# Layer 1's sliding-window attention: how many query panels are projected ahead of it, and how their split operands are laid out

## The chip, the cores and the metric

The kernel runs on one core of a Trainium2 chip. The core has five engines with instruction streams of their own, each in order: the tensor engine (PE), the vector engine (DVE), the scalar engine (ACT), GpSimd (POOL) and SyncE (SP), which here only starts transfers. The metric is the device time of one execution in microseconds (us). Lines are called L528 and so on; they are those of the kernel before unless the text says otherwise.

## The reference, cut to what matters

Two transformer layers over 512 latent tokens and 256 context tokens of width 1024, in float32. The change touches the attention of layer 1, which in the reference reads:

```python
def odd_mixer(a_lat, a_ctx, rows, cols, w_in, sinks, w_out, ctx_out):
    ...
    q, k, v = split(a_lat @ w_in, s)
    q = axial_rope(q, rows, cols)
    k = axial_rope(k, rows, cols)
    qc, kc, vc = split(a_ctx @ w_in, n_ctx)
    o_lat, o_ctx = swa_heads(q, k, v, qc, kc, vc, sinks, ctx_out)
    return o_lat @ w_out, (o_ctx @ w_out if ctx_out else None)
```

`w_in` gives 16 query heads of 64 columns, 2 key heads and 2 value heads; each key head serves 8 query heads. A latent query sees the latent keys within 128 positions and all 256 context keys in one softmax that also has a sink logit per head.

## The kernel before

**Arithmetic.** PE multiplies in a short format. So every operand is split in two: a high part (a cast, on ACT as a rule) and a low part (what the cast lost, a subtract on DVE as a rule). A projection then is three matmuls, high by high, high by low and low by high (L317, L319, L320). Tokens lie along the free dimension and features on the 128 partitions. `wr` is a raw weight panel, `wh` and `wl` its parts (L306, L307).

**The stage.** Before the change's place, layer 1's first products make keys `k32`, values `v32` and the queries of heads 0 and 1, `q0` (L738 to L740, then L317 to L320 for the context). Seven more query panels follow, one for each further pair of heads: `swa_queries(p)` loads 128 columns of `w_in`, multiplies them by the 512 normalised latents (24 matmuls of 512 columns into a `psd` bank), and rotates the result: an ACT copy (L447), a shuffle of partitions on DVE (L448), and three steps on POOL (L450, L451, L452). Then `put_q` splits the panel. A pair's two heads lie on partitions 0 to 63 and 64 to 127. The scores use all 128 rows of PE: for each head an operand `st` holds the high part of its query on its own 64 partitions and the low part on the other 64, and a key operand holds the key on both halves. So `put_q` runs twice over 64 partitions: a cast (L694) and a subtract that writes to the other half (L695). `put_k` makes, for each of the two key heads (`side`), the high operand (L708) and the low operand (L709) on one half and, with `copies` false, computes both again onto the other half (L714, L715); with `copies` true it moves them there by two transfers.

**The attention.** `swa_jobs` gives 16 jobs, two for each of 8 pairs of heads, each with two blocks of 128 queries. In a job each side (head) has scores against the context (4 matmuls of 256 columns into one `pss` bank) and against its window (2 of 256 or 384 columns for each block, L728 and L729). DVE adds the mask and takes the minimum (L538), ACT takes the exponential (L534), PE transposes the weights (L482) into `pst` or `psd` banks, DVE or ACT copies them out (L473, L474), and a run of weighted sums (L528) goes into `pso`, which ACT copies (L612). After a pair, `swa_finish` and `finish_pair` divide by the sums (L1618, L1619, L458, L461, L349, L465). `attend` interleaves the weighted sums of one job with the scores of the next. There are three `s`, two `t`, two `d` banks and one `o` bank; a panel and the transposes share the `d` banks.

**What sets the order.** The kernel is recorded and a scheduler places the instructions on each engine by priority. `beside` puts a generator in a queue of side work, `step` advances that queue by one step, `drain` empties it, and `shifted` lowers the priority of what it records. Here all seven panels are recorded ahead of the attention, 50 places lower (`LQ`), then drained; `EACH` is 0. The scheduler thus sets them near the front and pair 0's first jobs between them. Of the operand tiles `st` there are 12: four for the keys and two for each of four pairs.

## Time and profile before

| | |
|---|---|
| median of 3 runs | 1559.12 us (1555.52 to 1559.58) |
| profiled execution | 1558.19 us |
| its span, first to last instruction | 1556.3 us |
| granted TensorE clock | 0.996 |
| PE, DVE, ACT, POOL busy | 1529.0, 1176.5, 768.0, 217.0 us |
| the attention stage of layer 1, from panel 2 to the output projection | 998.7 to 1147 us |

The page gives, for each engine, the time in which any of its instructions ran. Matmuls overlap in the records: one starts while the last is still draining. So a busy PE can still lose time, and the distance between starts tells more than the busy share. "[0.24 <-ACT st L694]" behind a row says that the engine stood 0.24 us before it and that the cast on L694 let it go. A group's row ends with the same: idle time of the engine just before, and what ended it.

### The profile page before, as it was taken

How to read it: one execution, taken by the hardware profiler on the slowest of the kernel's cores; microseconds unless marked ns; L12 is line 12 of the kernel's file. 1: busy time of each engine (PE TensorE's matmuls, PEld its weight loads, DVE VectorE, ACT ScalarE, POOL GpSimd, SP SyncE). 2: the span in 40 equal slices, each digit the busy share in tenths (PEclk: the TensorE clock that was granted, in tenths of full speed). 3: DMA queues.
4: the chain of work that ended last, by engine and by line, in shares of the span. 5: the costliest groups of instructions: out<-in, count | busy, mean ns of one | idle time of the engine just before them, and what ended most of it. 6: DMA issues, size and time to landing. Idle time of an engine off the chain costs nothing.

```text
span 1556.3 us, 26589 instructions
## 1 busy us (share of the span) xinstructions
PE 1529.0 (98%) x10048; PEld 1374.9 (88%) x10048; DVE 1176.5 (76%) x2408; ACT 768.0 (49%) x1531; POOL 217.0 (14%) x269
## 2 busy tenths in 40 slices
PE   9999999999999999999999999999999999999998
PEld 8788877877999898999999988877789899899998
DVE  4799867676868687777768676789967779678685
ACT  4532677674555242432424335457856455354453
POOL 0021043110101102012021122470012000000001
PEclk9999999999999999999999999999999999999999
DMA  9674632013634545537465494110214223323222
GB/s 321 249 226 142 161 125 65 11 63 138 227 128 139 206 134 182 205 118 288 142 249 187 150 358 139 55 41 1 90 57 167 63 91 126 107 84 131 88 94 89
DMA packets 79073, 219.39 MB, mean 141 GB/s; under 512 B 10720, under 2 KB 17888, under 8 KB 78944
## 3 DMA queue, kind: packets, MB, share of 16 engines
q1 hardware_dynamic: 61280, 147.42, 28.6%
q0 software_dynamic: 16512, 68.69, 12.4%
q8 instruction: 79, 1.29, 0.3%
q10 hardware_dynamic: 1152, 1.57, 0.3%
q14 instruction: 50, 0.41, 0.1%
HBM read 186.97 MB, written 23.07 MB: 135 GB/s over the span
## 4 chain that ended last, share of the span: by engine, by line
PE 88%; DVE 7%; ACT 2%; issue 2%; DMA 1%; POOL 0%; DVEq 0%; ACTq 0%; POOLq 0%
PE pss L1401 5%; PE pss L1400 5%; PE pss L1399 5%; PE pso L528 5%; PE pss L320 4%; PE pss L317 4%; PE pss L319 4%; PE psd L317 4%; PE psd L320 4%; PE psd L319 4%; PE pst L317 3%; PE pst L320 3%; PE pst L319 3%; PE pst L1401 3%; PE pst L1399 3%; PE pst L1400 3%
## 5 line engine op out<-in xcount | busy, mean ns | idle before, releaser
L306 ACT CAST wh<-wr 128x1024 fp32r<-128x1024 f32 (+2 forms) x148 | 115.5, 795 | 224.2 <-DMA wr<-in_w_dn_dram 35.0
L307 DVE TENSOR_TENSOR wl<-wr,wh 128x1024 fp32r<-128x1024 f32 (+2 forms) x145 | 130.9, 910 | 80.6 <-ACT wh L306 76.3
L534 ACT ACTIVATE p<-p,sm 128x512 f32<-128x512 f32 (+3 forms) x144 | 105.0, 730 | 25.8 <-DVE sm L538 25.2
L1399 PE MATMUL pss<-b,wh 128*128 128x384 f32 (+1 forms) x346 | 107.7, 312 | 0.5 <-ACT b L343 0.5
L1400 PE MATMUL pss<-b,wh 128*128 128x384 f32 (+1 forms) x346 | 107.8, 312 | 0.0
L1401 PE MATMUL pss<-b,wl 128*128 128x384 f32 (+1 forms) x346 | 107.0, 311 | 0.0
L319 PE MATMUL psd<-b,wh 128*128 128x512 f32 (+2 forms) x254 | 88.6, 349 | 0.0
L273 DVE CUSTOM_DVE_ANT_0 p<-rope,cond 128x1024 bf16<-128x1024 f32 x64 | 76.8, 1219 | 11.4 <-DMA rope<-in_mod_w_dram 11.2
L317 PE MATMUL psd<-b,wh 128*128 128x512 f32 (+2 forms) x214 | 79.1, 370 | 2.8 <-ACT pl L474 2.2
L528 PE MATMUL pso<-ph,b 128*64 128x256 f32 (+1 forms) x384 | 77.9, 362 | 1.0 <-DVE ph L473 0.9
L528 PE MATMUL pso<-pl,b 128*64 128x256 f32 (+1 forms) x384 | 78.4, 363 | 0.0
L320 PE MATMUL psd<-b,wl 128*128 128x512 f32 (+2 forms) x214 | 77.5, 363 | 0.0
L1401 PE MATMUL pst<-b,wl 128*128 128x384 f32 (+1 forms) x226 | 70.6, 313 | 1.5 <-DVE wl L1387 1.5
L1386 ACT CAST wh<-pl 128x512 fp32r<-128x512 f32 x78 | 44.9, 619 | 53.6 <-PE pss L1400 22.7
L1399 PE MATMUL pst<-b,wh 128*128 128x384 f32 (+1 forms) x226 | 70.7, 313 | 0.6 <-ACT p L1449 0.6
L263 POOL DMA_DIRECT2D rope<-in_mod_w_dram x48 | 25.6, 533 | 323.0 <-DVE mod L273 312.1
L1400 PE MATMUL pst<-b,wh 128*128 128x384 f32 (+1 forms) x226 | 70.5, 312 | 0.0
L1386 ACT CAST wh<-wr 128x1024 fp32r<-128x1024 f32 x39 | 41.0, 1051 | 57.7 <-PE pst L1400 14.8
L319 PE MATMUL pss<-b,wh 128*128 128x256 f32 (+3 forms) x216 | 68.4, 316 | 0.0
L317 PE MATMUL pss<-st,wh 128*128 128x512 f32 (+2 forms) x198 | 67.5, 341 | 0.3 <-ACT wh L306 0.3
L320 PE MATMUL pss<-st,wl 128*128 128x512 f32 (+2 forms) x198 | 67.5, 341 | 0.1
L1399 PEld LDWEIGHTS pss<-b,wh 128*128 128x128 f32 x346 | 65.0, 188 | 1.1 <-ACT b L343 0.8
(606 smaller groups left out, 5290.7 us busy)
## 6 DMA issues: line engine op xcount, KB each, us to landing
wr<-in_w_gu_dram SPq DMA_DIRECT2D x88, 512.0 KB, 4.1
rope<-in_mod_w_dram POOLq DMA_DIRECT2D x48, 512.0 KB, 3.9
wr<-in_w_dn_dram SPq DMA_DIRECT2D x73, 256.0 KB, 2.9
wr<-in_w_out_dram SPq DMA_DIRECT2D x32, 512.0 KB, 3.9
p<-home POOLq DMA_DIRECT2D x40, 384.0 KB, 5.6
home<-p POOLq DMA_DIRECT2D x40, 384.0 KB, 5.9
wr<-in_w_in_dram SPq DMA_DIRECT2D x21, 512.0 KB, 3.9
ph<-in_mod_w_dram SPq DMA_DIRECT2D x24, 256.0 KB, 2.8
```

Of the source, the lines that this page charges most:

```text
L273: behind(V.tensor_tensor_reduce(out=T("p", [P, D], mybir.dt.bfloat16), in0=w, in1=cond[:, v, :], op0=ALU.mult, op1=ALU.add, scale=1.0, sca ...
L306: behind(S.copy(h, r), *after[:1])
L307: behind((G if eng else V).tensor_tensor(lo, r, f(h), op=ALU.subtract), *after[1:])
L317: ins = PE.matmul(o, wh[:, k], mh[:, c], start=first and k == 0, stop=False)
L319: PE.matmul(o, wh[:, k], ml[:, c], start=False, stop=False)
L320: PE.matmul(o, wl[:, k], mh[:, c], start=False, stop=last and k == n - 1)
L528: ins = PE.matmul(o[64 * i : 64 * i + 64, c], v(kt), t, start=n == 0, stop=n == len(moving[i]) - 1)
L534: S.activation(p[:, c], p[:, c], AF.Exp, bias=nm, scale=-1.0, accum_out=dn)
L1386: S.copy(h, t)
L1399: PE.matmul(o, wh, xh, start=first and k == 0, stop=False, skip_group_check=not first)
L1400: PE.matmul(o, wh, xl, start=False, stop=False, skip_group_check=not first)
L1401: PE.matmul(o, wl, xh, start=False, stop=k == 3, skip_group_check=not first)
```

## The change

Three things change together, all in layer 1.

1. Three panels (p = 1 to 3) are recorded ahead of the attention and drained; the other four are put beside it: when `swa_jobs` begins pair p below 4, it puts `swa_queries(p + 4)` into the side work. A pair whose operands are not recorded yet steps the side work until they are.
2. A panel is split once over all 128 partitions: one cast, one subtract in place, and three transfers on SP's queue that bring the halves to the other side.
3. The second key head's operands are recorded behind the three panels, at the lowered priority, and with `copies` true; the first head's stay as they are. Its two transfers go to POOL's queue, since `dense[0]` is true there.

```diff
-LQ, EACH = 50, 0
...
-    def put_k(ks, copies=True, hi=None):
+    def put_k(ks, copies=True, hi=None, only=(0, 1)):
+
+        sides = [(i, ks[i]) for i in only]
...
-            for side, (k1, k2) in enumerate(ks):
+            for side, (k1, k2) in sides:
...
     def swa_queries(p, every=1, get=PQ):
-        q, sets[p] = B(), new_q()
+        q, new = B(), new_q()
         yield from project(I["w_in1"][p], put_rope(q, rope1, SWAP16, scale=0.125), (LATS,), every=every, get=get)
-        put_q(sets[p], None, lo=V.tensor_tensor)(q[:, LATS], LATS)
+        q, (t0, t1) = q[:, LATS], (t[:, LATS] for t in new)
+        up, dn = slice(0, 64), slice(64, 128)
+        S.copy(t0, q)
+        lo = q.bitcast(F32R)
+        V.tensor_tensor(lo, q, f(t0), op=ALU.subtract)
+        dma(t1[up], t0[dn])
+        dma(t1[dn], lo[dn])
+        dma(t0[dn], lo[up])
+        sets[p] = new
...
-    put_k(KS, KC[2])(k32, slice(0, NT))
+    put_k(KS, KC[2], only=(0,))(k32, slice(0, NT))
...
         for p in range(8):
+            while p not in sets:
+                step()
+            if p < 4:
+                beside(swa_queries(p + 4))
             kv = p // 4
...
-    lower[0] = LQ
-    for p in range(1, 8):
+    lower[0] = 50
+    for p in range(1, 4):
         beside(swa_queries(p))
-        if EACH:
-            drain()
-            lower[0] += EACH
     drain()
     lower[0] = LOWER
+    with shifted(LOWER):
+        put_k(KS, only=(1,))(k32, slice(0, NT))
```

The order on all engines is the same ahead of this stage and from the last pair's end on; the number of PE instructions is the same, DVE and ACT have eight fewer each, SP has 21 more transfers and POOL two.

DVE's row where pair 0's attention begins, before. The tiles `b_10337` and `b_10382` are the rotated panels 1 and 2, `pss` the score banks, `wr` a weight panel; L695 are the subtracts over 64 partitions:

```order
L448 STREAM_SHUFFLE b_10417<-b_10416 128x512
L695 TENSOR_TENSOR st_10338<-b_10337,st_10338 64x512
L695 TENSOR_TENSOR st_10339<-b_10337,st_10339 64x512
L538 ISA p_10683,sm_10655<-pss_10675,zeros_92,sink_neg_10161 128x256
...
L307 TENSOR_TENSOR wl_10568<-wr_10565,wh_10567 128x1024
L448 STREAM_SHUFFLE b_10462<-b_10461 128x512
L695 TENSOR_TENSOR st_10383<-b_10382,st_10383 64x512
L695 TENSOR_TENSOR st_10384<-b_10382,st_10384 64x512
L538 ISA p_10683,sm_10655<-pss_10680,nb_10157,sm_10655 128x256
```

The same place after the change, with that kernel's own lines (L537 is L538 of before, L447 is L448, L306 is L307, L472 is L473); L1589 is the subtract over 128 partitions, `b_10333`, `b_10379` and `b_10425` are panels 1 to 3, `pss_10511` and `pss_10516` belong to pair 0's second side and `pss_10536` to its next job:

```order
L447 STREAM_SHUFFLE b_10414<-b_10413 128x512
L1589 TENSOR_TENSOR b_10333<-b_10333,st_10334 128x512
L537 ISA p_10519,sm_10478<-pss_10511,zeros_92,sink_neg_10161 128x256
...
L306 TENSOR_TENSOR wl_11044<-wr_11041,wh_11043 128x1024
L537 ISA p_10519,sm_10478<-pss_10516,nb_10157,sm_10478 128x256
...
L472 COPY ph_10580<-pst_10576 128x384
L1589 TENSOR_TENSOR b_10379<-b_10379,st_10380 128x512
L537 ISA p_10544,sm_10478<-pss_10536,zeros_92,sink_neg_10161 128x256
...
L1589 TENSOR_TENSOR b_10425<-b_10425,st_10426 128x512
L472 COPY pl_10553<-psd_10548 128x512
```

One subtract stands where two stood, and more of pair 0's reductions and copies stand between one panel's subtract and the next.

PE's row after pair 0's first side, before: panel 4 (`psd_10481`) ends, four scores, and panel 5 (`psd_10526`) begins:

```order
L319 MATMUL psd_10481<-b_10093,wh_10477 128x512
L320 MATMUL psd_10481<-b_10092,wl_10478 128x512
L728 MATMUL pss_10680<-st_10165,st_10171 128x256
L729 MATMUL pss_10680<-st_10166,st_10171 128x256
L728 MATMUL pss_10687<-st_10165,st_10171 128x384
L729 MATMUL pss_10687<-st_10166,st_10171 128x384
L317 MATMUL psd_10526<-b_10028,wh_10522 128x512
L319 MATMUL psd_10526<-b_10029,wh_10522 128x512
```

After (L729 and L730 are the scores, L481 the transposes, L316 to L319 the panel), panel 4 is `psd_10507`, and the scores are those of the same side, `pss_10516` and `pss_10526`:

```order
L729 MATMUL pss_10516<-st_10165,st_10171 128x256
L730 MATMUL pss_10516<-st_10166,st_10171 128x256
L316 MATMUL psd_10507<-b_10028,wh_10503 128x512
L318 MATMUL psd_10507<-b_10029,wh_10503 128x512
L729 MATMUL pss_10526<-st_10165,st_10171 128x384
L730 MATMUL pss_10526<-st_10166,st_10171 128x384
L481 MATMUL pst_10555<-ident_r_90,p_10487 128x128
L319 MATMUL psd_10507<-b_10028,wl_10504 128x512
L316 MATMUL psd_10507<-b_10045,wh_10503 128x512
L481 MATMUL pst_10555<-ident_r_90,p_10494 128x128
```

Panels 4 to 7 now stand among scores, transposes and weighted sums, the last of them beside pair 4.

DVE's row late in the attention after the change, beside pair 6, whose score banks are `pss_11737` and `pss_11773`. L464 (L465 of before) finishes a pair, `b_10834`, `b_11052` and `b_11237` being pairs 2, 3 and 4; L306 splits a panel of output weights:

```order
L464 TENSOR_TENSOR b_10834<-b_10834,pst_11644 128x512
L537 ISA p_11745,sm_11676<-pss_11737,zeros_92,sink_neg_10161 128x256
...
L464 TENSOR_TENSOR b_11052<-b_11052,pst_11665 128x512
L1628 TENSOR_TENSOR sm_11238<-sm_11238,sm_11723 128x8
...
L306 TENSOR_TENSOR wl_12193<-wr_12190,wh_12192 128x1024
...
L306 TENSOR_TENSOR wl_12228<-wr_12225,wh_12227 128x1024
L464 TENSOR_TENSOR b_11237<-b_11237,pst_11729 128x512
```

Before, a pair was finished beside the next one; now the finishing steps of pairs 2 to 5 stand in the last three pairs, because they queue behind the panels in the side work.

## The prediction

> **What bounds the kernel now.** I read the page first, then the busy time by stretches of the stage that the change touches, then the tensor engine (PE) instruction by instruction there, then what the vector engine (DVE) does in it. The page's head:
>
> ```profile
> span 1556.3 us, 26589 instructions
> PE 1529.0 (98%) x10048; PEld 1374.9 (88%) x10048; DVE 1176.5 (76%) x2408; ACT 768.0 (49%) x1531; POOL 217.0 (14%) x269
> ```
>
> PE is busy for 98% of the span, and the change takes no matmul away, so all that it can win is time in which PE stands. The stretches of layer 1 from the first matmul of query panel 2 to the first products of the output projection, with the columns PE, PEld, DVE, ACT, POOL, then clock, DMA share and GB/s:
>
> ```profile
> 998.70:1017.00 18.30, 18.30 (x86) 14.88 (x85) 17.54 (x24) 12.08 (x20) 13.72 (x8) 1.00 0.39 115
> 1017.00:1039.00 22.00, 21.68 (x110) 17.92 (x109) 15.15 (x32) 10.23 (x19) 19.74 (x14) 1.00 0.14 48
> 1039.00:1045.00 6.00, 4.78 (x38) 3.12 (x37) 5.87 (x17) 2.46 (x6) 3.12 (x3) 1.00 0.00 0
> 1045.00:1098.00 53.00, 52.49 (x428) 42.92 (x427) 50.18 (x170) 44.05 (x109) 0.00 (x0) 1.00 0.03 12
> 1098.00:1142.00 44.00, 43.72 (x357) 34.57 (x356) 38.72 (x133) 34.57 (x86) 0.00 (x0) 1.00 0.20 73
> 1142.00:1147.00 5.00, 4.32 (x38) 3.03 (x38) 3.90 (x7) 1.47 (x3) 0.00 (x0) 1.00 0.00 0
> ```
>
> The stage is 148.3 us. PE visibly stands 0.32 + 1.22 us while the panels end and the attention sets in, and 0.68 us at the end. DVE is slack beside the panels (15.15 of 22) and nearly full beside the attention (50.18 of 53). Busy hides more, because a matmul's record overlaps the next one's. The pace of the starts shows it (start, duration):
>
> ```profile
> 998.72 0.39 PE L317 MATMUL psd<-b,wh 128*128 128x512 f32 x1
> 998.95 0.39 PE L319 MATMUL psd<-b,wh 128*128 128x512 f32 x1
> ...
> 1050.54 0.28 PE L729 MATMUL pss<-st,st 128*128 128x256 f32 x1
> 1050.75 0.43 PE L528 MATMUL pso<-ph,b 128*64 128x256 f32 x1
> ...
> 1052.85 0.44 PE L482 MATMUL pst<-ident_r,p 128*128 128x128 f32 x2
> ...
> 1053.85 0.34 PE L729 MATMUL pss<-st,st 128*128 128x384 f32 x1
> 1054.02 0.28 PE L728 MATMUL pss<-st,st 128*128 128x256 f32 x1
> 1054.14 0.28 PE L729 MATMUL pss<-st,st 128*128 128x256 f32 x1
> ...
> 1055.05 0.60 PE L349 MATMUL pst<-ident_r,pl 128*128 128x128 f32 x4
> 1055.49 0.60 PE L482 MATMUL psd<-ident_r,p 128*128 128x128 f32 x4
> ```
>
> A panel matmul comes every 0.23 us, a score matmul every 0.12 (256 columns) or 0.17 (384), a transpose every 0.11 (four in 0.44), and a run of weighted sums (L528) takes 1050.54 to 1052.85 less one score, 2.19 us. The code issues in this stage 6 panels of 24, 16 jobs of 12 + 4 scores, 18 transposes and one run, and 8 times 4 spreads: 144 x 0.23 + 192 x 0.118 + 64 x 0.175 + 320 x 0.109 + 16 x 2.19 = 137 us, some 138 with the few others. So about 10 us of the 148.3 is PE waiting, most of it in gaps under 0.16 us that no row calls idle. The five or so waits before 1045 hide 0.16 us each: 1.54 + 0.8 = 2.3 us. The end has 1.0. That leaves 6.9 us over the 97 us of attention, where DVE and PE wait for each other in turn. **10 us, 0.65% of the kernel, is the ceiling of any gain.**
>
> **Part by part.** *Query parts on all partitions.* The subtracts of the low parts, alone and by group, with the key operands' two steps, and what else stands in DVE's row:
>
> ```profile
> 1013.41 3.40 DVE L695 TENSOR_TENSOR st<-b,st 64x512 fp32r<-64x512 f32 x2 [0.24 <-ACT st L694]
> 1019.87 2.40 DVE L695 TENSOR_TENSOR st<-b,st 64x512 fp32r<-64x512 f32 x2
> 1026.35 2.81 DVE L695 TENSOR_TENSOR st<-b,st 64x512 fp32r<-64x512 f32 x2 [1.17 <-ACT st L694]
> ```
>
> ```profile
> L307 DVE TENSOR_TENSOR wl<-wr,wh 128x1024 fp32r<-128x1024 f32 x13 | 15.8, 1236 | 3.0 <-ACT wh L306 3.0
> L695 DVE TENSOR_TENSOR st<-b,st 64x512 fp32r<-64x512 f32 x14 | 14.2, 1014 | 1.8 <-ACT st L694 1.4
> L473 DVE COPY ph<-pst 128x512 f32<-128x512 f32 x15 | 10.1, 679 | 0.0
> L448 DVE STREAM_SHUFFLE b<-b 128x512 f32<-128x512 f32 x7 | 5.2, 743 | 0.0
> L344 DVE TENSOR_TENSOR b<-b,st 128x512 fp32r<-128x512 f32 x8 | 5.0, 684 | 0.7 <-ACT st L343 0.7
> L715 DVE TENSOR_TENSOR st<-b,st 64x768 fp32r<-64x768 f32 x2 | 3.9, 1961 | 0.0
> L709 DVE TENSOR_TENSOR st<-b,st 64x768 fp32r<-64x768 f32 x2 | 2.2, 1124 | 0.4 <-ACT st L708 0.3
> ```
>
> Fourteen half-height subtracts cost 14.2 us: six beside the rotation on GpSimd (POOL) 8.6, 1.43 each, the other eight 0.70 each. Seven full-height ones take their place. A full-height subtract of the same width (L344) takes 0.68, so height costs nothing. Three still fall beside the rotation: 3 x 1.43 + 4 x 0.68 = 7.0, bounds 4.8 (all at 0.68) and 11.9 (all at 1.7, half of the 1013.41 pair). That takes 7.2 us from DVE. The key operands' second head loses one L715, 1.96. ScalarE sheds as many casts, and waits here anyway.
>
> By the Trainium skill (SBUF — State Buffer, Who interferes with whom) a DVE instruction with two SBUF inputs and a GpSimd instruction that reads SBUF hold one port by turns, and the loser waits for the other's whole instruction. If each of the three early subtracts waited out a rotation step of 2.17 us it would take 2.85, and the forecast below would be 4.3 us worse, 1561.5; the trace's worst pair, 3.40 for two, is milder.
>
> *Halves by transfer.* Seven times three transfers of 128 KB on SyncE's queue. Their like, over the whole kernel:
>
> ```profile
> st<-b SPq DMA_DIRECT2D x20, 96.0 KB, 2.2
> st<-st SPq DMA_DIRECT2D x7, 192.0 KB, 7.6
> ```
>
> The third transfer of a panel overwrites what the first one reads, so two stand in series: 4.4 to 15.2 us. I take 2.2 to 3 each, since 128 KB is nearer to 96 and SyncE's queue is almost empty here (DMA share 0.14 and 0.00 above). What hides it is the distance to the pair's first scores. For pair 1 that is closest. Its rotation and cast:
>
> ```profile
> 1006.50 2.01 POOL L450 TENSOR_TENSOR b<-b,rope 128x512 f32<-128x512 f32 x1 [2.90 <-DVE b L448]
> 1008.47 2.01 POOL L451 TENSOR_TENSOR b<-b,rope 128x512 f32<-128x512 f32 x1
> 1010.56 2.17 POOL L452 TENSOR_TENSOR b<-b,b 128x512 f32<-128x512 f32 x1
> ...
> 1030.27 1.30 POOL L450 TENSOR_TENSOR b<-b,rope 128x512 f32<-128x512 f32 x1
> ```
>
> ```profile
> 1012.75 1.26 ACT L694 CAST st<-b 64x512 fp32r<-64x512 f32 x2 [5.99 <-POOL b L452]
> ```
>
> Cast 0.63 and subtract 1.43 after 1012.7 make 1014.8, the transfers 1020. Panels 2 and 3, 48 x 0.23 us from 998.72, and a first side's scores end at 1011; the new order puts 24 panel matmuls (5.5), three sides' scores (3.2) and 16 transposes (1.7) before pair 1's first score, so it comes at 1021.5 or later: the cost is nothing, and 5 us or more if the transfers take 15. On SyncE the triples stand between output-weight loads that are needed 30 us later; panels 4 to 7 have 10 us and more of cover.
>
> *The start.* DVE's order moves so that attention comes before later panels' subtracts. Between the first scores of pair 0's second side and those of pair 1's second side, PE now has 24 x 0.23 + 4 sides x 1.06 (6 scores at 0.118, 2 at 0.175) + 26 x 0.109 = 12.6 us. In the same piece of DVE's row stand four sides of reductions, with this pace,
>
> ```profile
> 1009.35 0.48 DVE L538 CUSTOM_DVE_ANT_0 p<-pss,zeros,sink_neg 128x256 f32<-128x256 f32 x1
> ...
> 1010.16 1.40 DVE L307 TENSOR_TENSOR wl<-wr,wh 128x1024 fp32r<-128x1024 f32 x1
> ...
> 1011.48 0.47 DVE L538 CUSTOM_DVE_ANT_0 p<-pss,nb,sm 128x256 f32<-128x256 f32 x1
> ...
> 1012.43 0.73 DVE L448 STREAM_SHUFFLE b<-b 128x512 f32<-128x512 f32 x1
> ```
>
> two in 0.81 and two in 0.95, so 4 x 1.76 = 7.0, and two L307 (2.5), a shuffle (0.74), two subtracts (2.9), five copies (3.1, two of them narrower) and L709 (1.1): 17.3. Three score banks let PE run one side, 1.8 us, ahead. So PE waits 17.3 - 12.6 - 1.8, some 3 us, and longer where DVE stands before a subtract whose rotation is not done: 0 to 4 us (ScalarE stood 5.99 at that place), of which I take 0.5. That is 3.5 us (2.5 to 8) for today's 2.3: **+1.2**.
>
> *Beside the panels.* Panels 5 to 7, 72 x 0.23 = 16.6 us of PE, now lie inside pairs 1 to 4, the 53 us from 1045. DVE's 50 us there loses the late subtracts and faces 70 us: its share falls from 95% to about 70%. The gaps of that piece, 6.9 x 53 / 97 = 3.8 us, should mostly close; some is the price of changing from one kind of matmul to the next. I take **-3.0** (0 to -3.8). A panel holds one of the two d banks while it grows, which leaves the transposes three banks; that is the 0.8 I keep.
>
> *The last three pairs.* Finishing steps and splits of weights are pushed behind the panels. Between pair 5's first reduction and the last but one bank, DVE gets one L307, one shuffle, one subtract, one more multiply (as L344) and small steps: 1.24 + 0.74 + 0.9 + 0.68 + 0.6 = 4.1 us more, where PE in either order has 11 sides, 100 transposes, 5 runs and a dozen spreads, 35 us. DVE stood 44 - 38.7 = 5.3 us in the 44 us from 1098, so most of it fits. I take **+0.8** (0 to +4.1). The end, 1.0 us, stays.
>
> Sum: 1.2 - 3.0 + 0.8 = -1.0 us. The profiled execution took 1558.19 us (span 1556.3): **1557.2**. The median of the three runs is 0.06% above it, and they reach from 1555.5 to 1559.6; about 0.3%, 4.7 us, is what a measurement of this kernel can tell from no change.
>
> **The rivals.** *The two regimes really fit into each other* (25%): the start's waits shrink to 0.5 (-1.8), the middle wins 3.4, and the tail's extra goes into DVE's waits: -5.2, 1553.0. For it: DVE at 15 of 22 beside panels and 50 of 53 beside attention. Against: DVE's row is in order, and the early panels are still there. The Trainium skill (Perfetto Trace Analysis, Optimization Strategy) says that interleaving regimes with different most-contended engines may improve a kernel; by that rule this is the case, and the trace agrees as to the regimes.
>
> *DVE stands behind POOL* (10%): each of the first three subtracts waits for its rotation, because the rotations keep to 6.2 us a panel as at 1006.50 and not 3.9 (three at 1.30). Reductions queue behind them, PE waits 8 us at the start (+5.7), the banks hold back the middle (-1.5 only), tail +0.8: +5.0, 1563.2. It decides once DVE stands idle over 4 us in front of those subtracts. Against it: with DVE on PSUM work the rotation should run nearer to 1.3.
>
> *Halves late* (5%): two transfers in series over 9 us; PE waits up to 5 us at pair 1, part of it the 3.5 already counted: +2, 1559.
>
> **How the numbers follow.** The forecast, no change that can be told, has 60%. Range 1551.5 to 1562: from a little below the first rival, whose middle may win 3.8 and start 2.3, up to most of the second. Most of the first rival's chance lies beyond 4.7 us, most of the second's too, and the forecast's own tails add a little on both sides: faster 0.26, same 0.62, slower 0.12.
>
> **What would show it.** Right: PE's total count as before, DVE some 9 us less busy in the stage, 3 to 4 us of PE gaps between 1012 and 1032 with DVE full, a tight PE from there to the end of panel 7, and then waits on DVE copies. Wrong: no PE wait before 1032 (first rival), DVE idle in front of the subtracts (second), a score waiting for a DMA (third), or a stage under 143 us.

## The result, and the profile after

The changed kernel took 1562.16 us (median of 17 runs, 1559.93 to 1565.56), the kernel before 1559.58 us (17 runs, 1555.52 to 1562.26). The ratio is 1.0018 (95% interval 1.0010 to 1.0026): slower, by 2.6 us, where 1557.2 and no change that can be told was forecast. The profiled execution took 1562.23 us. (The profiled execution of one experiment below, dve_load2, ran PE at half its pace throughout; only its timed runs are used.) The engines' line of the page after; lines in the changed kernel differ by one from those before (L305 is L306 of before, L533 is L534, L481 is L482):

```profile
PE 1532.0 (98%) x10048; PEld 1377.2 (88%) x10048; DVE 1166.7 (75%) x2400; ACT 762.1 (49%) x1523; POOL 215.9 (14%) x271
```

DVE works 9.8 us less over the whole kernel (forecast: 9), and the kernel is slower all the same. The stretches of the stage (columns PE, PEld, DVE, ACT, POOL, clock, DMA share, GB/s):

```profile
998.16:1017.00 18.84, 18.84 (x97) 15.68 (x96) 16.84 (x33) 12.11 (x20) 14.83 (x9) 1.00 0.50 145
1017.00:1039.00 22.00, 20.41 (x126) 15.29 (x126) 17.29 (x54) 14.36 (x32) 8.07 (x8) 1.00 0.34 91
1039.00:1045.00 6.00, 6.00 (x46) 4.97 (x43) 4.23 (x15) 2.81 (x7) 0.00 (x0) 1.00 0.31 70
1045.00:1098.00 53.00, 52.72 (x392) 42.95 (x391) 38.27 (x134) 30.08 (x75) 7.64 (x6) 1.00 0.07 16
1098.00:1142.00 44.00, 42.49 (x342) 33.89 (x342) 40.27 (x134) 36.68 (x91) 4.84 (x3) 1.00 0.29 93
```

In these rows PE stands 1.6 us between 1017 and 1039, next to nothing while panels lie beside the attention, and 1.5 us in the 44 us from 1098, where it stood 0.3 before. All PE instructions of both traces are in the records and in the same number, so the stage can be measured between two that are the same in each kernel: the 6063rd matmul of the records, at the end of panel 1, and the 7171st, 7 us into the output projection. Before, these start at

```profile
997.79 0.39 PE L320 MATMUL psd<-b,wl 128*128 128x512 f32 x1
...
1154.18 0.27 PE L317 MATMUL pst<-st,wh 128*128 128x256 f32 x1
```

and after at the first and the last of these rows; the rows between them are read further down:

```profile
997.21 0.39 PE L319 MATMUL psd<-b,wl 128*128 128x512 f32 x1
...
1023.09 0.39 PE L729 MATMUL pss<-st,st 128*128 128x256 f32 x1
...
1024.42 0.33 PE L481 MATMUL pst<-ident_r,p 128*128 128x128 f32 x1 [0.28 <-ACT p L533]
...
1107.23 0.43 PE L527 MATMUL pso<-pl,b 128*64 128x256 f32 x1 [0.24 <-DVE pl L472]
...
1120.19 0.44 PE L481 MATMUL psd<-ident_r,p 128*128 128x128 f32 x2 [0.54 <-ACT p L533]
...
1156.01 0.27 PE L316 MATMUL pst<-st,wh 128*128 128x256 f32 x1
```

That is 156.4 us before and 158.8 after, +2.4, about what the medians differ by. The order is the same elsewhere; there the two traces differ by -0.6 us ahead of the stage and +2.3 behind it (1.2 of it up to the last matmul), as two executions of one order may.

From the starts of all matmuls in the stage, less nearly the paces that the prediction uses, come PE's waits. They are summed here from one job's run of weighted sums to the next one's: the first two jobs (pair 0, and the panels that stand ahead of it), jobs 3 to 10, jobs 11 to 15, and the rest. All kernels of the study, worked out in the same way; "ahead" is the number of panels ahead of the attention, and the column "torn" is explained below the table:

```
kernel         ahead parts  keys   stage  first two  3-10  11-15  rest   torn         ratio to before (95%)
before           7   half   ahead  156.4     3.3     4.2    2.4   1.2    11
full change      3   full   behind 158.8     4.7     3.9    3.4   1.2    2 4 10 13    1.0018 (1.0010-1.0026)
order_only       3   half   ahead  164.8     8.8     4.4    4.7   1.2    2 4 6 10 13  1.0057 (1.0039-1.0075)
parts_only       7   full   ahead  155.4     2.3     4.6    2.1   1.2    -            0.9997 (0.9985-1.0009)
keys_only        7   half   behind 158.5     4.5     5.5    2.2   1.2    -            1.0018 (1.0007-1.0028)
order_parts      3   full   ahead  160.5     6.4     4.0    3.4   1.2    2 4 10 13    1.0028 (1.0015-1.0042)
parts_keys       7   full   behind 157.0     2.3     6.1    2.2   1.2    -            1.0004 (0.9994-1.0014)
ahead4           4   full   behind 157.7     2.7     5.8    2.3   1.2    2 4 6 8 9    1.0010 (1.0000-1.0019)
ahead5           5   full   behind 153.4     0.9     4.0    1.8   1.2    2 4 6        0.9972 (0.9960-0.9984)
ahead6           6   full   behind 154.7     0.9     5.2    2.1   1.2    2            0.9993 (0.9982-1.0004)
ahead5_parts     5   full   ahead  154.7     1.3     4.6    2.1   1.2    2 4 6        1.0000 (0.9990-1.0011)
ahead6_parts     6   full   ahead  154.3     0.9     4.8    2.1   1.2    2            0.9991 (0.9981-1.0001)
steps5           3   full   behind 157.7     4.6     3.8    2.7   1.3    2            1.0014 (1.0004-1.0023)
finish_first     3   full   behind 160.9     4.7     4.3    5.1   1.2    2 4 6 10 12  1.0045 (1.0028-1.0063)
pool_cast3       3   full   behind 159.9     4.3     4.4    4.3   1.2    2 4 6 10 13  1.0024 (1.0015-1.0033)
no_sub3          3   full   behind 157.8     3.5     4.0    3.4   1.2    2 4 8 10 13  1.0022 (1.0013-1.0032)
no_rope3         3   full   behind 158.1     2.5     4.4    4.3   1.2    2 4 6 10 13  1.0015 (1.0005-1.0025)
dve_load         3   full   behind 158.3     4.2     3.9    3.4   1.2    2 4 10 13    1.0024 (1.0014-1.0034)
dve_load2        3   full   behind    no waits to be read                             1.0062 (1.0045-1.0078)
dve_load3        3   full   behind 164.1     4.7     8.3    4.4   1.2    2 6 10 13    1.0050 (1.0030-1.0070)
```

The paces weigh on such sums. Taken exactly as the prediction has them, the kernel before waits 3.7, 3.9, 2.3 and 1.2 us and the full change 5.0, 4.0, 3.3 and 1.2, so a figure of the table can be off by some 0.5 us.

Not all of it is waiting. "Torn" names the jobs whose run of weighted sums PE did in two pieces, with scores and transposes between them. A run is 20 matmuls that each take 64 of PE's 128 columns ("128*64" in the rows). Two partners start 0.007 us apart and run side by side, so a whole run has 10 starts; in a torn one, partners stand in different pieces, and it has 13. Job 10 before, where the run is whole, and after, where its second piece begins with the row of 1107.23 above:

```profile
1106.85 0.43 PE L528 MATMUL pso<-ph,b 128*64 128x256 f32 x1
1106.85 0.43 PE L528 MATMUL pso<-pl,b 128*64 128x256 f32 x1
...
1108.94 0.33 PE L482 MATMUL psd<-ident_r,p 128*128 128x128 f32 x1
```

```profile
1104.42 0.65 PE L527 MATMUL pso<-ph,b 128*64 128x256 f32 x2
1105.00 0.55 PE L481 MATMUL pst<-ident_r,p 128*128 128x128 f32 x3
...
1109.32 0.33 PE L481 MATMUL psd<-ident_r,p 128*128 128x128 f32 x1
```

A whole run took 2.10 us in every kernel where the clock was full, a torn one 0.58 + 2.09 = 2.67, and it takes 0.09 us more to enter its second piece: 0.66 us of PE's own time, which the table counts among the waits. (Job 6 of ahead5 and ahead5_parts is torn between two pairs: 10 starts, 0.24 us.)

So by the table the change moves the waits by +1.4, -0.3, +1.0 and 0.0 us; by the exact paces by +1.3, +0.1, +1.0 and 0.0, which adds up to the stage's 2.4. Of these, torn runs are +0.7, +1.3 and 0.0 (jobs 2, 4, 10 and 13 after, job 11 before): 2.0 of the 2.4 us. What is left as waiting moves by +0.6, -1.2, +1.0 and 0.0. The forecast had +1.2 at the start, -3.0 beside the panels, +0.8 in the last pairs and 0 at the end. Of the signs that it named, the gaps at the start came, with VectorE full (19.31 of the 20 us from 1012); the tight PE from there to the end of panel 7 did not.

What a wait at the start looks like: ScalarE's row after, around 1020 us and in the last pairs, and below it VectorE's:

```profile
1016.07 0.62 ACT L1587 CAST st<-b 128x512 fp32r<-128x512 f32 x1 [3.13 <-POOL b L451]
...
1020.29 0.62 ACT L1587 CAST st<-b 128x512 fp32r<-128x512 f32 x1 [2.07 <-POOL b L451]
1020.81 0.83 ACT L533 ACTIVATE p<-p,sm 128x640 f32<-128x640 f32 x1
...
1021.64 1.03 ACT L305 CAST wh<-wr 128x1024 fp32r<-128x1024 f32 x1
1022.69 0.83 ACT L709 CAST st<-b 64x768 fp32r<-64x768 f32 x1
1023.55 0.72 ACT L533 ACTIVATE p<-p,sm 128x512 f32<-128x512 f32 x1
...
1116.97 0.61 ACT L342 CAST st<-b 128x512 fp32r<-128x512 f32 x1
1117.48 1.05 ACT L305 CAST wh<-wr 128x1024 fp32r<-128x1024 f32 x1
1118.42 0.62 ACT L342 CAST st<-b 128x512 fp32r<-128x512 f32 x1
1118.94 0.49 ACT L1627 ACTIVATE sm<-sm,sink_bc 128x4 f32<-128x4 f32 x2
1119.33 0.72 ACT L533 ACTIVATE p<-p,sm 128x512 f32<-128x512 f32 x1
```

```profile
1011.52 1.13 DVE L1589 TENSOR_TENSOR b<-b,st 128x512 fp32r<-128x512 f32 x1 [1.61 <-ACT st L1587]
...
1020.39 0.47 DVE L537 CUSTOM_DVE_ANT_0 p<-pss,nb,sm 128x256 f32<-128x256 f32 x1
...
1105.49 1.21 DVE L306 TENSOR_TENSOR wl<-wr,wh 128x1024 fp32r<-128x1024 f32 x1
1106.62 0.55 DVE L472 COPY pl<-psd 128x384 f32<-128x384 f32 x1
...
1117.47 0.48 DVE L537 CUSTOM_DVE_ANT_0 p<-pss,nb,sm 128x256 f32<-128x256 f32 x1
```

ScalarE stood 3.13 and 2.07 us before the casts of panels 2 and 3, since GpSimd had not rotated them. The reduction of 1020.39 was done at 1020.9, but its exponential (512 columns) started at 1023.55: ahead of it in the row stood a weight's cast and the second key head's, neither needed soon. PE's transpose at 1024.42 waited for it. In the last pairs the reduction of 1117.47 was done at 1118.0, and its exponential stood behind two casts of finished pairs, one of an output weight and two steps of a finish until 1119.33; the transposes at 1120.19 waited for it. At 1105.49 a weight's subtract of 1.21 us stands ahead of the copy for which the run at 1107.23 waits. At the start ScalarE is not short of time (14.36 of the 22 us from 1017), and an instruction that PE needs stands behind some that it doesn't. In the last pairs ScalarE is short of it as well: from 1109.3 it was busy 4.10 of 4.10 us, and then (PE, PEld, DVE, ACT, POOL)

```profile
1113.40:1125.30 11.90, 10.84 (x84) 8.69 (x82) 11.32 (x37) 11.90 (x29) 0.00 (x0) 1.00 0.17 51
```

### The profile page after: what moved, and what is told of

The parts are those of the page before. It is cut to its first block, busy times and chain, and to the rows that moved or that the text cites. A ratio compares the mean times of both kernels' runs of the same rounds, so it can differ in the third digit from the quotient of the medians.

```text
span 1560.5 us, 26631 instructions
## 1 busy us (share of the span) xinstructions
PE 1532.0 (98%) x10048; PEld 1377.2 (88%) x10048; DVE 1166.7 (75%) x2400; ACT 762.1 (49%) x1523; POOL 215.9 (14%) x271
## 3 DMA queue, kind: packets, MB, share of 16 engines
q8 instruction: 79, 1.29, 0.3%
## 4 chain that ended last, share of the span: by engine, by line
PE 85%; DVE 6%; ACT 3%; DMA 3%; issue 2%; POOL 1%; DVEq 0%; ACTq 0%; POOLq 0%; SPq 0%
PE pss L1402 5%; PE pss L1401 5%; PE pss L1400 5%; PE pso L527 5%; PE psd L316 4%; PE pss L319 4%; PE psd L318 4%; PE pss L316 4%; PE psd L319 4%; PE pss L318 4%; PE pst L316 3%; PE pst L319 3%; PE pst L318 3%; PE pst L1402 3%; PE pst L1400 3%; PE pst L1401 3%
## 5 line engine op out<-in xcount | busy, mean ns | idle before, releaser
L305 ACT CAST wh<-wr 128x1024 fp32r<-128x1024 f32 (+2 forms) x148 | 115.5, 795 | 224.3 <-DMA wr<-in_w_dn_dram 45.2
L306 DVE TENSOR_TENSOR wl<-wr,wh 128x1024 fp32r<-128x1024 f32 (+2 forms) x145 | 131.6, 914 | 80.8 <-ACT wh L305 76.5
L533 ACT ACTIVATE p<-p,sm 128x512 f32<-128x512 f32 (+3 forms) x144 | 104.9, 730 | 31.3 <-DVE sm L537 31.1
L316 PE MATMUL psd<-b,wh 128*128 128x512 f32 (+2 forms) x214 | 79.3, 371 | 1.3 <-ACT pl L473 1.0
L319 PE MATMUL psd<-b,wl 128*128 128x512 f32 (+2 forms) x214 | 77.8, 364 | 0.0
L316 PE MATMUL pss<-st,wh 128*128 128x512 f32 (+2 forms) x198 | 67.5, 341 | 0.3 <-ACT wh L305 0.3
L319 PE MATMUL pss<-st,wl 128*128 128x512 f32 (+2 forms) x198 | 67.6, 341 | 0.1
```

The source lines that it names most:

```text
L305: behind(S.copy(h, r), *after[:1])
L306: behind((G if eng else V).tensor_tensor(lo, r, f(h), op=ALU.subtract), *after[1:])
L316: ins = PE.matmul(o, wh[:, k], mh[:, c], start=first and k == 0, stop=False)
L319: PE.matmul(o, wl[:, k], mh[:, c], start=False, stop=last and k == n - 1)
L533: S.activation(p[:, c], p[:, c], AF.Exp, bias=nm, scale=-1.0, accum_out=dn)
```

## The experiments

The theory after the first reading: the order costs, because at the start exponentials queue behind casts and because late panels and finishing steps crowd the last pairs. Rivals: the new parts cost (a cast behind the rotation, or late halves); the late keys cost; each rearrangement is a new deal whose parts don't add up.

### The three parts of the change, alone and in twos

order_only puts back the old parts and both key heads ahead:

```diff
-    put_k(KS, KC[2], only=(0,))(k32, slice(0, NT))
+    put_k(KS, KC[2])(k32, slice(0, NT))
...
-        S.copy(t0, q)
...
+        put_q(sets[p], None, lo=V.tensor_tensor)(q[:, LATS], LATS)
...
-    with shifted(LOWER):
-        put_k(KS, only=(1,))(k32, slice(0, NT))
```

> Only the order: three panels ahead and four beside the attention; query parts by half-height steps and both key heads' operands ahead, as in the kernel before. Theory (the order costs, since exponentials queue behind casts in ScalarE's row at the start and the last panels and finishing steps fall among the last pairs): at least as slow as the full change, +2.5 to +5 us on the kernel before. First rival (the new query parts cost, by a cast that stands behind the rotation or by late halves): 0 +-1 us. Second rival (each rearrangement deals a new order, and the parts don't add up): anything within +-2 us.

Measured: 1.0057, stage +8.4 us, above the theory's range; both rivals fall. Some 1.6 us of it, at the start, are a stretch of half clock in this execution (last section); the order costs more than forecast without it too.

parts_only records all seven panels ahead again, and both key heads:

```diff
-            while p not in sets:
-                step()
-            if p < 4:
-                beside(swa_queries(p + 4))
...
-    for p in range(1, 4):
+    for p in range(1, 8):
...
-    with shifted(LOWER):
-        put_k(KS, only=(1,))(k32, slice(0, NT))
```

> Only the new query parts (full-height cast and subtract, halves by transfer); all seven panels ahead, both key heads' operands ahead. Theory: VectorE loses some 9 us beside the panels, where it is slack, so -0.5 +-0.7 us on the kernel before. First rival (the parts cost): +2 us or more. Second rival: within +-2 us.

Measured: 0.9997 (0.9985 to 1.0009), stage -1.0 us, as the theory has it. The new parts don't cost; the first rival falls.

keys_only records seven panels ahead with the old parts, and leaves the second key head behind them:

> Only the second key head's operands behind the panels, halves by transfer; all seven panels ahead, old query parts. Theory: 0 +-0.7 us, since no score of the second head is due before pair 4. Third rival (its casts and subtracts, now placed among the first pairs' exponentials and reductions, hold these up): +1 us or more. Second rival: within +-2 us.

Measured: 1.0018, stage +2.1 us: 1.2 at the start, 1.3 in jobs 3 to 10. The 1.2 are not the keys'. Where pair 0's first run of weighted sums stands, PE's order is that of the kernel before, but the granted clock was low in this execution:

```profile
1037.50:1042.20 4.70, 4.70 (x28) 3.06 (x28) 3.53 (x11) 1.85 (x5) 0.12 (x1) 0.64 0.00 0
```

The same matmuls, from a first score to the first score behind the run of weighted sums, took 4.68 us here and 3.06 before: 1.6 of the 2.1 us. That leaves 0.5 us of stage, within the theory's 0 +-0.7, while the times (+2.8 us) side with the rival of the late keys. The second head's cast and subtract stand at 1077 to 1081 us, and jobs 8 and 9 right behind them wait 0.4 and 0.8 us longer than before.

Two parts at a time: order_parts leaves out the keys' move, parts_keys the order.

> The order and the new query parts; both key heads' operands ahead of the panels, as in the kernel before. So far the stage from the first matmul of panel 2 to the end of the last pair's products took, in each profiled run, 156.4 us before, 158.8 with the full change, 164.8 with the order alone, 155.4 with the parts alone, 158.5 with the keys alone. Theory (the start is bound by what stands in the rows of VectorE and ScalarE there): the second head's cast and subtract, 0.8 and 1.0 us, leave the start, so 157.8, one us less than the full change. Rival (the keys cost their 2.1 us wherever they stand): 156.7. Rival (every new order is a new deal): above 158.8 is possible too.

Measured: 1.0028, stage 160.5, 1.7 us *above* the full change; theory and rivals but the last missed. The rows tell why. VectorE's and ScalarE's rows in order_parts at pair 0's first reductions:

```profile
1006.65 0.95 DVE L710 TENSOR_TENSOR st<-b,st 64x768 fp32r<-64x768 f32 x1
1007.62 1.95 DVE L716 TENSOR_TENSOR st<-b,st 64x768 fp32r<-64x768 f32 x1
1009.61 0.48 DVE L537 CUSTOM_DVE_ANT_0 p<-pss,zeros,sink_neg 128x256 f32<-128x256 f32 x1
```

```profile
1013.01 0.62 ACT L1587 CAST st<-b 128x512 fp32r<-128x512 f32 x1 [5.97 <-POOL b L451]
1013.65 1.28 ACT L533 ACT_TABLE_LOAD   x1
1014.95 0.72 ACT L533 ACTIVATE p<-p,sm 128x512 f32<-128x512 f32 x1
```

The second head's two subtracts stand 2.9 us ahead of the first reductions, and the first exponential stands behind a cast that waits 5.97 us for GpSimd. From the first pair's end on its PE order is that of the full change, and the waits of jobs 3 to 15 are the same to 0.02 us each. So the move of the keys costs some 0.5 us of stage by itself (2.1 less the clock's 1.6) and 1.6 beside the new parts, and saves 1.7 with three panels ahead: where an instruction stands decides.

> All seven panels ahead, with the new query parts and the second key head behind the panels. If the parts of the change add up: stage -1.0 + 2.1 = 157.5 us. If the keys cost because they stand among the first pairs where VectorE is full, and the new parts make room there: 156.0 to 156.5. New deal: anything between 155 and 159.

Measured: 1.0004, stage 157.0 us, between the first two forecasts.

### The last pairs

steps5 and finish_first change one line each:

```diff
-STEPS = ((2, 3, 4, 4), 5, 3)
+STEPS = ((2, 3, 4, 4), 5, 5)
```

```diff
-            beside(then)
+            (side_work.appendleft if phase[0] == 2 else beside)(then)
```

> The changed kernel with five instead of three steps of side work for each attention job of layer 1, so that panels 4 to 7 end by pair 4 and the finishing steps are not pushed behind them. Theory: the last pairs' extra waits (1.7 us) go, and the start stays: 1 to 2 us faster than the changed kernel. Second rival: within +-2 us of it, with no tie to the last pairs' waits; if the panels merely crowd earlier pairs, what the end wins comes back between pairs 1 and 4 and the time stays.

Measured: stage 157.7, 1.1 us less than the full change, 0.7 of it in jobs 11 to 15 (1.0014 to the full change's 1.0018, which the times alone would not tell apart). The size is as expected, the reason is not: three runs fewer are torn, 2.0 us, and without the torn runs jobs 11 to 15 wait as long (2.5 against 2.6) and jobs 3 to 10 1.0 longer.

> The changed kernel with each pair's finishing step put at the front of the side work, not behind the panels. Theory (1.0 us of the waits among the last pairs come from finishing steps that pile up there behind panel 7): stage 157.5 to 158, about 1 us less than the full change's 158.8. Rival (panel 7's own steps and the output weights make those waits, and pushing panels later makes them worse): 158.8 or more.

Measured: 1.0045, stage 160.9, 2.1 us more; jobs 11 to 15 wait 5.1 instead of 3.4. The theory falls as to the sum, and its rival holds: panel 7 came in jobs 9 and 10 instead of 8 and 9. But the wait for which finishing steps had stood ahead of an exponential did go: job 12 has 0.2 us in place of 2.3 (without its torn run). Job 13 has 1.5 in place of 0.1: its transposes wait for a copy that stands in ScalarE's row behind panel 7's cast and an exponential, and that cast waited for the rotation:

```profile
1126.02 0.62 ACT L1587 CAST st<-b 128x512 fp32r<-128x512 f32 x1 [1.16 <-POOL b L451]
```

Jobs 14 and 15 wait 0.9 and 0.8 longer too. So finishing steps and panel 7's own steps both cost where they come late; no run takes away one without moving the other.

### The start

pool_cast3 moves a cast, and no_sub3 and no_rope3 leave work of panels 1 to 3 out:

```diff
-        S.copy(t0, q)
+        (G.tensor_copy if p < 4 else S.copy)(t0, q)
```

```diff
-        V.tensor_tensor(lo, q, f(t0), op=ALU.subtract)
+        if p > 3:
+            V.tensor_tensor(lo, q, f(t0), op=ALU.subtract)
```

```diff
...
+            S.activation(x[:, LATS], src, AF.Copy, scale=scale)
+            V.stream_shuffle(y[:, LATS], x[:, LATS], mask=swap)
+            G.tensor_tensor(q[:, c], x[:, LATS], y[:, LATS], op=ALU.add)
...
```

> The full change with the cast of panels 1 to 3's query parts on GpSimd, right behind the rotation, in place of ScalarE. Theory (at the start ScalarE's row stands before these casts until the rotation is done, and exponentials queue behind it): the start's waits fall from 4.7 us to 3.7 or less; stage 157.8 or less. Rival (VectorE's row is what is late there, and its subtract now waits for a longer GpSimd row): 4.7 or more, stage 158.8 to 161.

Measured: the first two jobs wait 4.3 us, 0.4 less. That is no more than in dve_load, where nothing of the start was changed and its order fell out a little differently (4.2); stage 159.9. Inconclusive.

> The full change without the subtract of panels 1 to 3 (the low part of their queries is then the whole query, so the output is another one). If the start is bound by the amount in VectorE's row: 3.5 us less there, the first two jobs' waits fall from 4.7 us to 2 or less. If it is bound by the rotation on GpSimd, for which ScalarE's casts wait with the exponentials behind them: 4.0 to 4.7.

Measured: 3.5 us, 1.2 less.

> The full change with one rotation step on GpSimd in place of three for panels 1 to 3 (their queries are then not rotated rightly, so the output is another one). VectorE and ScalarE keep all their steps, and the rotation ends 3 us and more sooner in each panel. If the start is bound by the amount in VectorE's row: 4.0 to 4.7 of waits in the first two jobs. If it is bound by the rotation, for which casts and exponentials behind them stand: 2 or less.

Measured: 2.5 us, 2.2 less. No bound of either expectation was met: both the rotation and what stands in VectorE's row have a share, the rotation the larger. (Some 0.5 us between starts is what a chance order makes, as in dve_load; and with fewer rotation steps the three subtracts took 3.0 us in place of 3.5, so a little of the 2.2 is VectorE's row as well.)

### How many panels ahead

```diff
-            if p < 4:
-                beside(swa_queries(p + 4))
+            if p < 2:
+                beside(swa_queries(p + 6))
...
-    for p in range(1, 4):
+    for p in range(1, 6):
```

This is ahead5; ahead4 and ahead6 change the same numbers, ahead5_parts and ahead6_parts leave out the keys' move as well.

> The changed kernel with six panels ahead and one beside the attention instead of three and four. Theory (waits at the start come from pairing early attention with panels whose rotation is not done, waits at the end from panel 7 and the finishing steps behind it): start 2 to 3 us of waits instead of 4.7, and the one panel falls in pairs 0 and 1, so the last pairs lose their extra 1.0: stage 156 to 156.8. Rival (work of panels beside the attention is what fills VectorE's waits, and fewer panels there give that back): 158 or more.

> The full change with five panels ahead and two beside the attention. So far in three ahead the waits of the first two jobs are 4.7 us (stage 158.8), in six ahead 0.9 (154.7), in seven ahead 2.3 (157.0). Theory (the price at the start comes with few panels ahead, and at the end with late panels): start 1 to 3, stage 155 to 157. Rival (each order is a new deal, with no trend): outside of that.

> The full change with four panels ahead and three beside the attention. The first two jobs' waits were 4.7 us with three ahead, 0.9 with five, 0.9 with six, 2.3 with seven. Each panel more ahead brings PE 5.6 us and VectorE some 3 (a weight split 1.2, a shuffle 0.7, a subtract 0.7 to 1.7), so 2.6 us of the wait goes: about 2, and the last pairs' waits lie between 3.4 (three) and 1.8 (five): stage 155 to 157. Rival (each order is a new deal): outside of that.

Measured, from three to seven ahead: the first two jobs wait 4.7, 2.7, 0.9, 0.9 and 2.3 us, the stage takes 158.8, 157.7, 153.4, 154.7 and 157.0. All three missed their ranges: ahead6 came out 1.3 us under 156 to 156.8, ahead5 1.6 under 155 to 157 and ahead4 0.7 over, with 5.8 us in jobs 3 to 10, where four of its runs are torn. The start follows the number of panels up to five, the stage does not, and seven ahead starts worse than five; so for ahead5 and ahead4 the rival of a new deal (outside of the ranges) holds. ahead5 beats both kernels: 0.9972 (0.9960 to 0.9984). Its stretches to the end of job 2 and of job 10:

```profile
997.10:1048.60 51.50, 51.50 (x289) 42.07 (x287) 39.15 (x95) 30.08 (x57) 32.30 (x22) 1.00 0.39 104
1048.60:1105.60 57.00, 56.29 (x455) 45.59 (x454) 51.65 (x171) 41.85 (x104) 4.65 (x4) 1.00 0.11 28
```

PE stands nowhere in the first, with the same rotations and the same casts behind them: two more panels give it matmuls meanwhile.

> Six panels ahead and one beside the attention, new query parts, both key heads' operands ahead as in the kernel before. Theory (the second head's late steps cost 1.5 us in the order with seven ahead, and cost nothing ahead where four more panels stand between them and the first reduction): stage 153.5 to 154.7, 2 to 3 us less than before; the total 0.15 to 0.2% below. Rival (as with three ahead, they hold up the first reductions by 1.7 us): 156 or more.

> Five panels ahead and two beside the attention, new query parts, both key heads' operands ahead. With six ahead the keys ahead saved 0.4 us against the keys behind, with three ahead they cost 1.7. With five the first jobs' waits were 0.9 us with the keys behind: if three more panels than in the three-ahead order are cover enough for the keys' 2.9 us of VectorE work, 153 to 153.5 us; if not, 154.5 to 155.

Measured: ahead6_parts 154.3 us as expected, 0.4 less than ahead6 (its time, 0.9991, is 0.09% below where 0.15 to 0.2 was expected, with 1 inside the interval); ahead5_parts 154.7, 1.3 more than ahead5, and 1.0000. The keys' place is worth either sign again, and in time the gain of five ahead came only with them behind.

### Whether the small waits follow VectorE's share

```diff
+            if 8 < more[0] <= 40:
+                with shifted(LOWER):
+                    V.tensor_tensor(T("more", [P, 384]), rope1[:, 0, :384], rope1[:, 1, :384], op=ALU.mult)
```

> The full change with 32 more VectorE multiplies (128x384, about 0.5 us each, of no use to the output) among the attention jobs 3 to 10, four to a job, at low priority: some 17 us of VectorE work in the stretch where four panels lie. The prediction's step (the small waits there follow VectorE's share, 95% before and about 75% after): the share comes back to that of before, and the waits of jobs 3 to 10, 3.9 us after the change, grow by about 3: stage 161.5 to 162. Rival (they don't follow its share; the order in which the steps stand makes them): 3.9 +-1, stage 158 to 160.

Measured: nothing on the question, since the 32 multiplies, tied to nothing, ran ahead of the stage, from 932.5 to 980.7 us. From the second job on it has the full change's order, and repeats its waits: 3.9 and 3.4 us. dve_load2 ties each multiply behind a reduction of its job, and dve_load3 leaves out one in four:

> As the run before with 32 more VectorE multiplies (128x384, 0.55 us each, of no use to the output), but each tied behind a reduction of the attention jobs 3 to 10, where the earlier ones had all run before the stage. They are some 17.6 us of VectorE work in the 69 us of those jobs, whose VectorE share is 75% with the full change and 94% in the kernel before. The prediction's step (the small waits follow VectorE's share): they grow from 3.9 us by about 3. Rival (the order in which the steps stand makes them, whatever VectorE's share): 3.9 +-1.

Measured: 1.0062 (1.0045 to 1.0078), no waits to be read.

> The full change with 24 more VectorE multiplies (128x384, 0.55 us each, of no use to the output), three to a job behind reductions of the attention jobs 3 to 10: 13.2 us, which brings VectorE's share there from 75% to some 94%, as in the kernel before. (With 32, which fill it, the time rose to 1.0062 of the kernel before, but its profiled execution ran TensorE at half its pace and shows no waits.) The prediction's step (the small waits follow VectorE's share): 3.9 us of waits grow by about 3. Rival (they don't, as the kernel before has them tight at 94%): 3.9 +-1.

Measured: 1.0050 (1.0030 to 1.0070), and 8.3 us in jobs 3 to 10, 4.4 more. Jobs 3 to 10 in it, in the full change and in the kernel before (PE, PEld, DVE, ACT, POOL):

```profile
1041.60:1114.00 72.40, 69.87 (x506) 55.14 (x505) 61.72 (x201) 41.95 (x103) 10.81 (x9) 1.00 0.10 23
```

```profile
1040.60:1109.30 68.70, 67.98 (x507) 55.15 (x506) 51.68 (x179) 40.31 (x101) 12.49 (x9) 1.00 0.09 22
```

```profile
1052.80:1108.90 56.10, 55.53 (x453) 44.82 (x451) 52.53 (x173) 44.41 (x107) 0.00 (x0) 1.00 0.03 11
```

The share was 85%, not 94: the jobs themselves became longer. The rival's 3.9 +-1 fails, and the growth is more than the prediction's step had (about 3). The run also dealt a new order (jobs 11 to 15, without any load, wait 1.0 longer), so a part of the 4.4 may be that.

By the table the share tells nothing: 94% goes with 4.2 us, 75% with 3.9 and 85% with 8.3. But the table's figure holds the torn runs. Without them, and by the exact paces, jobs 3 to 10 wait 2.2 to 2.7 us in the six orders where VectorE's share is 74 to 78% (2.7 with the full change), 3.7 and 3.3 at 80 and 81% (steps5, ahead4), and 3.0 to 5.8 in the eight orders at 86 to 94% (3.9 before); with the added load 7.0. So these waits go with VectorE's work, with a wide scatter that the share does not tell. The six orders at the low end are also those with the most panel matmuls in the stretch; only the added load speaks for VectorE alone.

## Why the prediction was wrong

**Query parts: right.** Seven subtracts took 6.3 us (forecast 7.0, bounds 4.8 to 11.9) in place of 14.2, and one L716 is gone. VectorE's groups in the stage, after:

```profile
L1589 DVE TENSOR_TENSOR b<-b,st 128x512 fp32r<-128x512 f32 x7 | 6.3, 895 | 2.7 <-ACT st L1587 2.6
...
L716 DVE TENSOR_TENSOR st<-b,st 64x768 fp32r<-64x768 f32 x1 | 2.0, 1959 | 0.0
```

The longest of the three beside the rotation took 1.68 us, not the 2.85 that the prediction worked out. By the Trainium skill (SBUF — State Buffer, Who interferes with whom) one instruction waits out the other. The trace agrees (last section), and the 2.85 was wrongly worked out: its 2.17 was a step that had itself been waiting for VectorE (the row of 1010.56, behind the weight's subtract of 1010.16), while a step that runs takes 1.29 us.

**Halves by transfer: right.** A transfer landed in 2.2 to 2.3 us (forecast 2.2 to 3):

```profile
st<-b SPq DMA_DIRECT2D x6, 128.0 KB, 2.2
st<-st SPq DMA_DIRECT2D x3, 128.0 KB, 2.3
```

Panel 1's came right behind its cast and its subtract (1011.52), and pair 1's first score at 1023.09 (forecast 1021.5 or later). No score waited for a transfer.

**The start: right in size by luck, half right in kind.** +1.3 to +1.4 us against +1.2, but 0.7 of it is job 2's torn run, which the sum didn't have. The sum was over VectorE's row, which was full there, and no_sub3 shows that its length counts (1.2 of 4.7 us). But most of PE's named waits there (0.9 of 1.6 us) are for exponentials, and no_rope3 shows the larger share (2.2): ScalarE's row stands behind GpSimd's rotation. The second rival had this idea with VectorE as the engine that stands; there it stood once, 1.61 us. And the sum's own rule, PE's time against VectorE's, points to more panels ahead: each brings PE 5.6 us and VectorE some 3, and the waits fell by 2.0 and 1.8 with the fourth and the fifth. It doesn't tell why they rose again to 2.3 with seven.

**Beside the panels: wrong, and the step that failed.** "The gaps of that piece, 6.9 x 53 / 97 = 3.8 us, should mostly close": 3.0 us were taken; 0.3 came by the table and none by the exact paces. The amount of work fell as said, DVE's share from 94 to 75%. Two things failed.

One is a term put at nothing, 1.3 of the 3.1 us missing here. The sum has "16 x 2.19" for the weighted sums, one price per run whatever the order, and 0.8 us kept for the change between kinds of matmul and the banks. With panels among the jobs PE does some runs in two pieces: 2.85 us with both entries and not 2.19. Jobs 4 and 10 lost 1.3 us in this way, and the stage 2.0 us net. Of the four kernels with all seven panels ahead only the kernel before has a torn run, one; those with six have one, those with three to five have three to five (steps5: one). What made the scheduler tear just these is open: no run kept the order and left the runs whole.

The other is a size, 1.8 us. The waits proper fell by 1.2 us, not 3.0. The prediction spread them evenly over 97 us, while they sit in certain jobs: before, jobs 3 to 10 waited 0.10, 0.72, 0.10, 0.32, 1.15, 0.56, 0.43 and 0.83 us. After, the panels' matmuls lay in jobs 2, 3, 5, 6, 8 and 9, and these were tight there (0.38, 0.09, 0.11, 0.09, 0.12 from the third on), but of the 4.2 us before only 1.5 lay in jobs that got a panel. Jobs 4, 7 and 10 waited 1.16, 0.50 and 1.48, with a torn run in the first and the last. And 75% is an average. By job, VectorE's share fell to 35 and 50% in jobs 5 and 8; in jobs 4, 7 and 10 it was 99, 91 and 93% before and still 87, 88 and 92% after. Jobs 5 and 10 after (PE, PEld, DVE, ACT, POOL):

```profile
1058.00:1066.10 8.10, 8.10 (x53) 6.29 (x52) 2.84 (x10) 3.58 (x10) 0.00 (x0) 1.00 0.22 49
...
1101.00:1109.30 8.30, 7.86 (x61) 6.09 (x59) 7.61 (x24) 5.23 (x14) 4.84 (x3) 1.00 0.16 48
```

So the cover went mostly to jobs with little to lose. The reason given, VectorE's work, has the runs on its side as to direction (dve_load3, and the orders compared without torn runs). It is not the whole: jobs 6 and 9, at 83 and 89%, were tight, and some waits are for a single instruction that stands behind others in a row (the copy at 1106.62).

**The last pairs: right in size (+1.0 against +0.8), half right in kind.** The sum was over VectorE's row, while ScalarE's was full for the 16 us from 1109.3: casts of finished pairs and of output weights and finishing steps stand ahead of exponentials. That the finishing steps are part of it, as the prediction said, finish_first bears out for job 12; that panel 7's late place costs as well, for job 13.

**The sum.** By the exact paces 1.3 + 0.1 + 1.0 = 2.4 us, where -1.0 was forecast (by the table 1.4 - 0.3 + 1.0 = 2.1); 3.1 of the 3.4 us between them are the middle term. "The two regimes fit" did not come with three panels ahead; by the Trainium skill (Perfetto Trace Analysis, Optimization Strategy) interleaving may help, and here it did with five ahead (-3.0 us of stage) and cost with three.

## What to carry to other kernels

Ask first whether PE does the same matmuls in the same time: time each run of them before and after, since an order that parts two partners costs PE's own time, which looks like waiting. Then work out an engine's share job by job, not over the stretch, and count only the waits in those jobs that get the cover; look up, at each wait, which instruction stands ahead of the one that is late in its row. When work is moved beside a chain, sum each engine's row for the first piece as well as PE's time there, and measure the neighbours of the number chosen (here five ahead was better than three, four and six). Parts of a change that are placed by a scheduler don't add up; measure them together, by the same two instructions in each trace, and look at the granted clock between them.

## What the runs showed of the hardware

Beside VectorE's weight splits and subtracts, with two operands in SBUF, a rotation step on GpSimd took up to 2.30 us and not 1.29, and the subtract up to 1.68 and not 0.69. Whichever begins later waits for the rest of the other. From 998 to 1034 us, in both traces, each of the 14 rotation steps that began beside such a VectorE instruction ended 1.14 to 1.17 us behind that one's end, and each of the seven subtracts of 512 columns that began beside such a step ended 0.55 us behind the step's. Two steps after, and the weight's subtract that began beside the first:

```profile
1005.92 1.29 POOL L449 TENSOR_TENSOR b<-b,rope 128x512 f32<-128x512 f32 x1 [2.88 <-DVE b L447]
1007.17 2.30 POOL L450 TENSOR_TENSOR b<-b,rope 128x512 f32<-128x512 f32 x1
```

```profile
1006.46 1.83 DVE L306 TENSOR_TENSOR wl<-wr,wh 128x1024 fp32r<-128x1024 f32 x1
```

It waited for the first step (ended 1007.21) and ended at 1008.29; the second step waited for it and ended at 1009.46.

In order_only, where PE stood 4.0 of 22 us, the granted clock of that stretch was 0.92; before and after it was 1.00 there. Right behind a wait of 2.26 us, scores of 256 columns came every 0.21 us and not 0.12 for some 3.4 us:

```profile
1017.00:1039.00 22.00, 18.04 (x112) 14.61 (x113) 21.14 (x56) 15.56 (x35) 7.47 (x6) 0.92 0.16 48
```

In keys_only the same came behind a wait of 0.94 us, and in the kernel before, behind one of 0.81, it did not; two cases don't give a rule.

Two weighted sums that take 64 columns each and start 0.007 us apart ran side by side, and 20 of them took 2.10 us as ten pairs and 2.67 with 13 starts.

One order of instructions in two programs (full change and dve_load, from the second job on) gave the same waits to 0.02 us in each job, while the times of single executions scatter by 0.2%: where the clock is the same, the stage in a trace tells apart what medians of eleven and 17 runs don't (steps5 and the full change).
